# Taking GpSimd's low parts and state sums of the second mixer over to VectorE

## The chip, the cores and the metric

The kernel runs on one core of one Trainium2 chip. The metric is the device time of one execution in microseconds (us), and the time before is the median of three runs. The engines are TensorE (PE in the rows, PEld for its weight loads), VectorE (DVE), ScalarE (ACT), GpSimd (POOL) and SyncE (SP), which issues nearly all transfers here. Each engine takes its instructions in program order; engines wait for one another through semaphores.

## The reference, cut to what matters

The reference is an encoder trunk of two layers over 512 positions of width 1024, in float32. Layer 0 has a mixer of windowed attention and gated linear attention; layer 1 has the second mixer, which is the place of this change. Both are followed by cross-attention into 256 memory tokens and a gated feed-forward block.

```python
def mixer_cd(hn, w_in, w_out, ...):                     # the second mixer
    u_c, h_d = split_sizes(hn @ w_in, (C_WIDTH, 2 * D_WIDTH))
    y_f = s5_scan(u, ...)                                # a linear recurrence, forward
    y_b = flip(s5_scan(flip(u), ...))                    # and backward
    y = y_f + y_b + d_skip * u_c
    z = gelu(y)
    o_c = z * sigmoid(z @ w_glu + b_glu)
    o_d = conformer_conv(h_d, conv_w, ...)               # 31 taps, layer norm, silu
    return concatenate([o_c, o_d]) @ w_out
```

What is computed stays the same under the change: `a - b` and `a + b` of the same tiles are done on another engine.

## The kernel before, in words

**Weights in two parts.** Every large product is done with operands that are split into a high and a low part. `wload` (line 194) takes a raw block of 128x1024 weights (`wr`, fetched by line 147 through SP, 3 buffers), rounds it on ScalarE to the high part `wh` (line 201), and subtracts that from the raw block on VectorE, or on the engine that it is given, to get the low part `wl` (line 202). `mm3` then issues three matmuls for each 128x128 block: line 206 (high weights, high input), line 207 (high weights, low input) and line 208 (low weights, high input). So the first two can start once `wh` is there, and the third waits for `wl`. (Where the weights are the moving operand, as in the memory's value projection, line 207 is the one that reads `wl`.) `wh` and `wl` have two buffers each, and a raw block is free for the next transfer when both parts have been made.

**The second mixer.** `mixer_cd` runs a table of small steps, `CD`, in the order written there; `pinned` keeps the first TensorE and SP instruction of each step in that order. On VectorE and ScalarE the order comes from a list scheduler that estimates durations, so it can move rows there when an instruction changes its engine. The steps that matter here:

- `u`, `v`, `g` and `k`: products with the weights of the input projection (`half0` and `half1`) and with the memory's key and value weights (`vstep`, `kstep`). Each takes one block of weights through `wload`. The numbers in `LPOOL` name the blocks whose low part GpSimd makes.
- `c`, `C`, `s`, `x`: the linear recurrence of one group, forward (d = 0) and backward (d = 1). `c_` multiplies the input with the table on TensorE, copies it out on ScalarE, swaps its halves with two transfers, rotates it (lines 1380 to 1382), scans it (lines 1384 and 1386) and rotates it back (lines 1387 and 1388). `s_` has SP swap the halves of the result with four transfers (lines 1394 and 1395), and SP takes them in order with all other transfers: what stands behind them, the next weights among it, is issued only when line 1388 of both directions has ended. `x_` (line 1402) adds the two halves to the state `xp`; the numbers in `XPOOL` name the sums that GpSimd makes.
- `q`: taps of the convolution on VectorE (line 1463), 60 in all, which nothing on TensorE waits for soon.
- `V` and `G`: the gate and value of the convolution (lines 1440, 1445 and 1447), whose result TensorE transposes in `A` (line 1336).
- `N`: the layer norm of the convolution. VectorE adds up squares (line 1520), TensorE sums them over partitions (line 1522), ScalarE and VectorE make the factor from it (lines 244 to 247), VectorE applies it (line 1576), and the result, split into `cm` and `cst` tiles, is the second half of the input of the output projection.

The functions that take the two tables, and what calls them:

Of the kernel before, what the change touches and what calls it, by code (L numbers as in the profile page):

```python
# [75 lines left out]
S5_EVERY = 3  # L76
RAW = ((1, 3), (1, 5))
NPRE = 2
LPOOL, XPOOL = (5, 6, 7, 15, 18, 19, 20, 22, 24, 26), (1, 2, 6)
WAHEAD = 2  # L80
NQ = 2
CD = """
# [1651 lines left out]
```

## Time and profile before

| | |
|---|---|
| median of 3 runs | 1613.68 us (1609.65 to 1622.86) |
| the profiled execution | 1613.46 us, its span 1611.7 us |
| mean granted TensorE clock | 0.984 |
| busy, share of the span | PE 97%, PEld 81%, DVE 67%, ACT 44%, POOL 22% |
| the second mixer | about 861 us to 1100 us of the span |

The span runs from the first to the last instruction; 1.8 us of the execution's time lie outside it. All positions below are microseconds from the start of the span. A row of the timeline gives the start, the duration, the engine, the line, the operation, the output and its inputs, and, in square brackets, how long the engine sat idle before it and for whom.

### The profile page before, as it was taken

What the parts mean: (1) busy time and instruction counts of PE and PEld (TensorE: products, weight loads), DVE (VectorE), ACT (ScalarE), POOL (GpSimd) and SP (SyncE); (2) the same over time, 40 slices, a digit from 0 to 9 for tenths busy, and PEclk for the clock granted to TensorE, in tenths of its full rate; (3) what the DMA queues carried; (4) which work ended last, traced back from release to release, by engine and by line L of the source; (5) the groups of instructions that cost most, each with busy time, mean ns of one, the idle gap of its engine ahead of it and who ended that gap; (6) DMA issues with size and microseconds to landing.
All of it is one profiled execution on the core that took longest, in us unless ns stands there. A gap on an engine that the chain in (4) does not pass through costs nothing. (4 is left out here: it accounts for less than half of the span.)

```text
span 1611.7 us, 20961 instructions
## 1 busy us (share of the span) xinstructions
PE 1562.1 (97%) x8036; PEld 1307.9 (81%) x8036; DVE 1077.3 (67%) x1479; ACT 708.3 (44%) x1089; POOL 358.7 (22%) x367
## 2 busy tenths in 40 slices
PE   8999999999999999999999988989999999999997
PEld 6787889888888787777788877978888888888887
DVE  7576766466568789579746997375745766636644
ACT  5464755354444443234336342374534444414423
POOL 8411000000059853553510111110000101100101
PEclk9999999999999999999999998999999999999998
DMA  5322333231223335435454685452302322232331
GB/s 178 109 72 86 118 105 118 66 121 63 66 80 100 111 111 152 144 116 164 126 166 172 218 276 172 150 177 91 106 27 79 105 97 100 92 105 92 89 109 64
DMA packets 76117, 189.11 MB, mean 117 GB/s; under 512 B 8368, under 2 KB 27440, under 8 KB 76016
## 3 DMA queue, kind: packets, MB, share of 16 engines
q1 hardware_dynamic: 75376, 186.58, 36.1%
q8 instruction: 63, 1.03, 0.3%
q0 software_dynamic: 320, 1.05, 0.2%
q14 instruction: 38, 0.31, 0.1%
q10 hardware_dynamic: 320, 0.13, 0.0%
HBM read 162.43 MB, written 19.01 MB: 113 GB/s over the span
## 5 line engine op out<-in xcount | busy, mean ns | idle before, releaser
L201 ACT ACTIVATE wh<-wr 128x1024 fp32r<-128x1024 f32 (+1 forms) x229 | 239.2, 1045 | 430.3 <-PE mm L207 324.2
L208 PE MATMUL mm<-hg,wl 128*128 128x512 f32 x1000 | 394.9, 395 | 12.3 <-DVE wl L202 10.9
L206 PE MATMUL mm<-hg,wh 128*128 128x512 f32 x1000 | 399.2, 399 | 4.6 <-ACT wh L201 4.6
L207 PE MATMUL mm<-hg,wh 128*128 128x512 f32 x1000 | 393.6, 394 | 0.0
L202 DVE TENSOR_TENSOR wl<-wr,wh 128x1024 fp32r<-128x1024 f32 (+1 forms) x219 | 285.7, 1305 | 73.7 <-ACT wh L201 71.6
L208 PEld LDWEIGHTS mm<-hg,wl 128*128 128x128 f32 x1000 | 190.3, 190 | 56.6 <-DVE wl L202 13.7
L206 PEld LDWEIGHTS mm<-hg,wh 128*128 128x128 f32 x1000 | 190.7, 191 | 46.5 <-ACT wh L201 5.0
L207 PEld LDWEIGHTS mm<-hg,wh 128*128 128x128 f32 x1000 | 190.4, 190 | 40.4 <-issue 1.4
L208 PE MATMUL mm<-g,wl 128*128 128x512 f32 x324 | 126.7, 391 | 3.2 <-DVE wl L202 3.1
L206 PE MATMUL mm<-g,wh 128*128 128x512 f32 x324 | 126.9, 392 | 0.0
L207 PE MATMUL mm<-g,wh 128*128 128x512 f32 x324 | 126.2, 389 | 0.0
L976 POOL TENSOR_TENSOR t<-t,t 128x512 f32<-128x512 f32 x22 | 28.9, 1315 | 427.6 <-ACT t L182 427.6
L968 DVE TENSOR_TENSOR u<-mm,R 128x512 f32<-128x512 f32 x88 | 60.3, 688 | 73.8 <-PE mm L208 73.6
L970 ACT ACTIVATE t<-u,vt 128x512 f32<-128x512 f32 x88 | 70.8, 807 | 42.9 <-DVE u L968 42.6
L986 DVE TENSOR_TENSOR h<-mm,h 128x512 f32<-128x512 f32 x40 | 27.6, 691 | 87.7 <-PE mm L208 87.7
L971 DVE SCALAR_TENSOR_TENSOR t<-u,vt,t 128x511 f32<-128x511 f32 x88 | 77.8, 885 | 7.9 <-ACT t L970 7.9
L972 DVE SCALAR_TENSOR_TENSOR t<-u,vt,t 128x511 f32<-128x511 f32 x88 | 76.8, 872 | 4.0 <-DMA dct<-tr 1.4
L208 PEld LDWEIGHTS mm<-g,wl 128*128 128x128 f32 x324 | 60.8, 188 | 16.8 <-DVE wl L202 4.0
L182 ACT ACTIVATE t<-t 128x512 f32<-128x512 f32 x44 | 27.8, 632 | 102.3 <-DVE t L972 102.2
L207 PEld LDWEIGHTS mm<-g,wh 128*128 128x128 f32 x324 | 60.8, 188 | 12.5
L206 PEld LDWEIGHTS mm<-g,wh 128*128 128x128 f32 x324 | 60.9, 188 | 12.4
L202 POOL TENSOR_TENSOR wl<-wr,wh 128x1024 fp32r<-128x1024 f32 x10 | 25.3, 2531 | 148.4 <-ACT wh L201 148.4
(522 smaller groups left out, 3020.2 us busy)
## 6 DMA issues: line engine op xcount, KB each, us to landing
wr<-in_w_up SPq DMA_DIRECT2D x88, 512.0 KB
wr<-in_w_dn SPq DMA_DIRECT2D x32, 448.0 KB
wr<-in_w_ab SPq DMA_DIRECT2D x16, 512.0 KB
wr<-in_w_xv SPq DMA_DIRECT2D x16, 512.0 KB
wr<-in_w_xk SPq DMA_DIRECT2D x16, 512.0 KB
wr<-in_w_xq SPq DMA_DIRECT2D x16, 512.0 KB
wr<-in_w_xo SPq DMA_DIRECT2D x16, 512.0 KB
wr<-in_w_dn SPq DMA_DIRECT2D x16, 512.0 KB
```

The costliest lines, as they stand in the source:

```text
L182: tabbed(A.activation(dst, src, fn, **kw))
L201: A.activation(H[:, :n], raw[:, :n], AF.Copy)
L202: (eng or V).tensor_tensor(L[:, :n], raw[:, :n], H[:, :n].bitcast(F32), ALU.subtract)
L206: PE.matmul(ps, lH, rH, start=start, stop=False)
L207: PE.matmul(ps, lH, rL, start=False, stop=False)
L208: PE.matmul(ps, lL, rH, start=False, stop=stop)
L968: V.tensor_tensor(u, ps, R, ALU.mult)
L970: A.activation(t, u, AF.Identity, scale=vc(f"cw{l}", 44 + i), bias=vc(f"cb{l}", i))
L971: V.scalar_tensor_tensor(t[:, 1:], u[:, :S - 1], vc(f"cw{l}", i), t[:, 1:], op0=ALU.mult, op1=ALU.add)
L972: V.scalar_tensor_tensor(t[:, :S - 1], u[:, 1:], vc(f"cw{l}", 88 + i), t[:, :S - 1], op0=ALU.mult, op1=ALU.add)
L976: (V if l == 0 else G).tensor_tensor(res[1], res[1], res[0], ALU.mult)
L986: V.tensor_tensor(h[c], ps, h[c], ALU.add)
```

## The change

Two tables of numbers become empty:

```diff
@@ -76,7 +76,7 @@
 RAW = ((1, 3), (1, 5))
 NPRE = 2
-LPOOL, XPOOL = (5, 6, 7, 15, 18, 19, 20, 22, 24, 26), (1, 2, 6)
+LPOOL, XPOOL = (), ()
 WAHEAD = 2
 NQ = 2
```

With them, ten low parts of weights (line 202, 128x1024) and three sums of scanned states (line 1402, 128x512) go from GpSimd to VectorE. GpSimd keeps its few memsets (lines 1273 to 1278) in this mixer. SP's 460 rows stay as they are. TensorE and ScalarE have the same rows as before, with some of them in another order, and VectorE has 13 rows more. Three places follow.

VectorE in the scan of the third group: `T_1276` and `T_1280` are its two directions, `dv_7578` is the convolution's sum over taps, and `wl_7908` is a low part of the input projection's weights.

```order
 L1382 TENSOR_TENSOR T_1276_7726<-T_1276_7726,T1s_7727 128x512
 L1327 TENSOR_TENSOR uT_7802<-mm_7777,R_7356 128x512
+L202 TENSOR_TENSOR wl_7908<-wr_7771,wh_7907 128x1024
+L1463 SCALAR_TENSOR_TENSOR dv_7578<-dv_7424,vt,dv_7578 128x506
 L1382 TENSOR_TENSOR T_1280_7749<-T_1280_7749,T1s_7750 128x512
+L1384 SCALAR_TENSOR_TENSOR T1s_7727<-rt_7714,T_1276_7726 128x512
 L1463 SCALAR_TENSOR_TENSOR dv_7578<-dv_7424,vt,dv_7578 128x507
-L1384 SCALAR_TENSOR_TENSOR T1s_7727<-rt_7714,T_1276_7726 128x512
```

The low part now stands between the two directions' sums, and the rows of the scan are behind it. Two of the three state sums (`xp_7309` and `xp_7308`) come into VectorE's rows near here in the same way, one ahead of this piece and one behind it.

TensorE at the sum over partitions of the layer norm, line 1522 (`sc_8853`), among the key products of the memory (`mm_8989`, `mm_9022`). Before:

```order
L206 MATMUL mm_8989<-mg_7487,wh_8985 128x256
L207 MATMUL mm_8989<-mg_7487,wh_8985 128x256
L1522 MATMUL sc_8853<-T_1459_8838,ones 128x512
L206 MATMUL mm_9022<-mg_7487,wh_9018 128x256
L207 MATMUL mm_9022<-mg_7487,wh_9018 128x256
L208 MATMUL mm_8989<-mg_7487,wl_8986 128x256
```

Now:

```order
L207 MATMUL mm_8989<-mg_7765,wh_8985 128x256
L208 MATMUL mm_8989<-mg_7765,wl_8986 128x256
L1522 MATMUL sc_8853<-T_1459_8838,ones 128x512
L206 MATMUL mm_9022<-mg_7487,wh_9018 128x256
L207 MATMUL mm_9022<-mg_7487,wh_9018 128x256
L208 MATMUL mm_9022<-mg_7487,wl_9019 128x256
```

The sum over partitions now comes behind the whole product `mm_8989`, 22 matmuls later.

VectorE behind it, where the layer norm's factor is made and applied; `wl_9128` and `wl_9147` are low parts of the output projection's first two blocks:

```order
 L245 SCALAR_TENSOR_TENSOR T1s_9199<-sc_8853,T1s_9199 128x512
 L246 TENSOR_SCALAR T1s_9199<-T1s_9199 128x512
+L202 TENSOR_TENSOR wl_9128<-wr_9125,wh_9127 128x1024
 L247 TENSOR_TENSOR dg_9197<-T_1523_9198,T1s_9199 128x512
+L851 TENSOR_TENSOR kraw_9077<-mm_9083,Rm_8117 128x256
+L202 TENSOR_TENSOR wl_9147<-wr_9144,wh_9146 128x1024
 L1576 TENSOR_TENSOR dv_7578<-dv_7578,dg_9197 128x512
 L1576 TENSOR_TENSOR dv_7841<-dv_7841,dg_9197 128x512
```

Both low parts now stand ahead of the four products of line 1576; before, they came behind them.

## Rows read from the trace of the kernel before

**Rows 1.** The page, part 1: busy us (share of the span) and instructions.

```profile
PE 1562.1 (97%) x8036; PEld 1307.9 (81%) x8036; DVE 1077.3 (67%) x1479; ACT 708.3 (44%) x1089; POOL 358.7 (22%) x367
```

**Rows 2.** Windows of the mixer: length, busy by engine, granted clock, DMA.

```profile
950.00:970.00 20.00, 13.84 (x70) 9.98 (x69) 19.96 (x30) 9.51 (x17) 4.89 (x2) 0.93 0.89 324
970.00:990.00 20.00, 20.00 (x138) 18.14 (x139) 9.60 (x13) 4.49 (x6) 0.00 (x0) 0.90 0.21 52
990.00:1010.00 20.00, 16.62 (x88) 13.16 (x87) 19.96 (x25) 6.67 (x10) 4.28 (x2) 0.91 0.66 234
...
1080.00:1100.00 20.00, 20.00 (x82) 16.32 (x82) 10.26 (x13) 9.74 (x13) 0.00 (x0) 0.92 0.48 175
sum 260.00, PE 244.01 PEld 206.60 DVE 187.81 ACT 118.48 POOL 30.21; mean PE 16.27 PEld 13.77 DVE 12.52 ACT 7.90 POOL 2.01
```

**Rows 3.** Waits of TensorE from 860 to 1080: total us, times, longest.

```profile
PE mm L206 <- ACT wh L201: 3.5, 1, 3.5
PE mm L208 <- POOL wl L202: 3.3, 2, 1.8
PE tp L1336 <- DVE dv L1447: 2.8, 1, 2.8
PE mm L208 <- DVE wl L202: 1.8, 1, 1.8
PE sc L1522 <- DVE T L1520: 1.7, 1, 1.7
```

**Rows 4.** Lines 202 and 1402 in the mixer: ns minimum/median/maximum.

```profile
L202 DVE TENSOR_TENSOR wl<-wr,wh x18: 1203/1219/1590, 871.1 to 1071.5; 128x1024 fp32r<-128x1024 f32 x18
...
L202 POOL TENSOR_TENSOR wl<-wr,wh x10: 2353/2399/3380, 879.7 to 1068.1; 128x1024 fp32r<-128x1024 f32 x10
...
L1402 DVE TENSOR_TENSOR xp<-T,X2s x5: 672/677/1769, 903.5 to 1006.7; 128x512 f32<-128x512 f32 x5
```

**Rows 5.** Timeline of GpSimd, three of its 13 operations.

```profile
903.47 1.28 POOL L1402 TENSOR_TENSOR xp<-T,X2s 128x512 f32<-128x512 f32 x1 [21.31 <-DMA X2s<-T1s]
913.82 3.38 POOL L202 TENSOR_TENSOR wl<-wr,wh 128x1024 fp32r<-128x1024 f32 x1 [9.08 <-ACT wh L201]
...
1000.25 2.62 POOL L202 TENSOR_TENSOR wl<-wr,wh 128x1024 fp32r<-128x1024 f32 x1 [30.48 <-ACT wh L201]
```

**Rows 6.** Timeline of VectorE at the same moments and between them.

```profile
903.52 1.77 DVE L1402 TENSOR_TENSOR xp<-T,X2s 128x512 f32<-128x512 f32 x1
...
915.51 2.24 DVE L1382 TENSOR_TENSOR T<-T,T1s 128x512 f32<-128x512 f32 x1
...
927.23 1.78 DVE L1463 SCALAR_TENSOR_TENSOR dv<-dv,vt,dv 128x511 f32<-128x511 f32 x1
...
935.96 0.73 DVE L1463 SCALAR_TENSOR_TENSOR dv<-dv,vt,dv 128x501 f32<-128x501 f32 x1
...
1000.54 2.86 DVE L1463 SCALAR_TENSOR_TENSOR dv<-dv,vt,dv 128x504 f32<-128x504 f32 x1
1003.33 1.74 DVE L1447 SCALAR_TENSOR_TENSOR dv<-dg,dv 128x512 f32<-128x512 f32 x1
...
1059.06 2.62 DVE L1520 TENSOR_TENSOR T<-T,X2s 128x512 f32<-128x512 f32 x1 [0.17 <-ACT X2s L1519]
```

**Rows 7.** Timeline at the late block of weights: SP, ScalarE, TensorE.

```profile
958.23 0.46 SPq L1394 DMA_DIRECT2D X2s<-T1s  x1
...
966.08 1.06 ACT L201 ACTIVATE wh<-wr 128x1024 fp32r<-128x1024 f32 x1 [3.32 <-DMA wr<-in_w_cd]
...
969.83 0.80 PE L208 MATMUL mm<-hg,wl 128*128 128x512 f32 x1 [1.42 <-POOL wl L202]
```

**Rows 8.** The chain of waits, in order of time: start, us, what.

```profile
1070.89 0.12 PE mm L206
...
1079.49 0.23 PE mm L208
...
1081.23 0.43 PE mm L207
```

## The prediction, put on record before the result was known

> **What bounds the kernel now.** The page's first part says that TensorE is busy for 97% of the span and VectorE for 67% [rows 1], so the kernel as a whole is TensorE's, and an engine that is freed or loaded elsewhere counts only where TensorE stands still. I therefore read the windows of the second mixer next. From 860 to 1100 us there are 260.00 us less 244.01 busy, 16 us, in which TensorE does nothing, and in the windows that hold most of them VectorE is the full engine: 19.96 of 20 us from 950 to 970, and again from 990 to 1010 [rows 2]. This is the stage to look at, not VectorE's 67%. The waits of TensorE name what it stood still for: a high part of weights (3.5 us), low parts from GpSimd (3.3), the gated value of the convolution from line 1447 (2.8), a low part from VectorE (1.8), the last sum of squares (1.7) [rows 3]. That makes 13.1 of the 16 us.
>
> Last I laid the timelines of GpSimd and VectorE side by side, because the change turns on them. GpSimd needs 2.40 us for a low part where VectorE needs 1.22 [rows 4]. While GpSimd runs, the VectorE row that falls into it grows: the state sum at 903.52 takes 1.77 us where its median is 0.68; a sum of the same size at 915.51 takes 2.24 and ends when GpSimd's row of 913.82 is over; a tap at 1000.54 takes 2.86 where one takes 0.73 [rows 4 to 6]. So GpSimd's work here is not beside VectorE's but in it. It works the other way as well: GpSimd's low part at 913.82, among VectorE's rows, takes 3.38 us [rows 5].
>
> **The change, part by part.** Ten low parts at 1.22 and three sums at 0.68 are 14.2 us more rows on VectorE [rows 4], against the time by which rows no longer grow. What matters is the sum on the three paths that end in a wait of TensorE.
>
> Place 1, from 900 to 970. TensorE waits for a high part that ScalarE makes at 966.08, and ScalarE had waited 3.32 us for the block of weights [rows 7]. That block is late because SP issues it behind the swaps of the scanned states; the last two were issued from 958.23 on [rows 7], once line 1388 had ended, and VectorE had then been full since 900. On VectorE up to there, the change takes away the growth of three rows: 1.77 − 0.68 = 1.09, 2.24 − 0.68 = 1.56 and 1.78 − 0.73 = 1.05, together 3.70 us [rows 4, 6]. It puts in one low part and two sums, 1.22 + 2 × 0.68 = 2.58 [rows 4]. So the swaps, the block of weights and the high part come 1.1 us earlier: 966.08 becomes 965.0. The high part is there 1.06 later, at 966.0, and VectorE makes the low part in 1.22, at 967.3, where TensorE's first matmul with it started at 969.83 [rows 7]. The gain is **2.6 us**. It holds the 1.4 us wait for GpSimd's low part. Bounds: 1.1 if VectorE is not free when the high part is there, 3.5 + 1.4 = 4.9 if both waits vanish.
>
> A rule bears on this. The Trainium skill, "SBUF — State Buffer", section "Who interferes with whom", says that a VectorE instruction with two SBUF inputs and a GpSimd instruction that reads SBUF exclude each other for the whole instruction, and that whichever starts first holds the other up. By it the sum of 915.51 is held until GpSimd's end at 913.82 + 3.38 = 917.20, so for 1.69 us where the rows give 1.56 [rows 5, 6]; the one at 903.52 for 1.23 where they give 1.09. Put on three rows, the rule would make place 1 some 0.4 us better. The same rule speaks against the change where VectorE starts first: there GpSimd pays and VectorE loses nothing, as GpSimd's 3.38 us in part show. The sum here goes by the rows.
>
> Place 2, from 990 to 1010. TensorE waits 2.8 us for line 1447 [rows 3]. That row takes 1.74 instead of 0.68, and the tap in front of it 2.86 instead of 0.73 [rows 4, 6]: 1.06 + 2.13 = 3.2 us of growth right ahead of the wait, while the low part and the state sum that take GpSimd's place stand behind line 1447 in VectorE's new order. The gain is the whole wait, **2.8 us**. Bounds: 0 if a transfer ahead of the scan sets the time, 2.8.
>
> Place 3, from 1058 to 1080. Three waits lie here: 1.7 for line 1520, 1.8 for GpSimd's second low part, 1.8 for VectorE's low part behind the products of line 1576 [rows 3], 5.3 in all. The first goes, as line 1520 took 2.62 us [rows 6] and TensorE now has 22 matmuls ahead of line 1522. The second goes, as the low part is made in half the time. The third goes, as the low part now stands ahead of line 1576. Something is late in their place: line 1522 comes 22 matmuls of 0.12 us [rows 8] later, 2.6, less the 1.7 that it no longer waits, so 1.0 us later, and the layer norm behind it with the `cm` tiles that the output projection needs. The low part ahead of line 1576 adds up to 1.2 to that [rows 4], but TensorE gets ten matmuls of the second block to do first, 10 × 0.23 = 2.3 us [rows 8], so I count the 1.0 alone: **4.3 us**. Bounds: 5.3, and 0 if the `cm` tiles come no earlier than before and TensorE, ahead by 5.3, waits for them.
>
> The other moves cost nothing: from 1010 to 1050 TensorE has no wait in the list of [rows 3] and VectorE stands idle, so two low parts more fit in; the memsets of GpSimd stay. SP's queue is in the same order, and its weight transfers that waited for GpSimd to release a raw block can only be earlier.
>
> The granted clock is the other half. The windows at 0.93, 0.90, 0.91 and 0.92 [rows 2] are stretches at 1.2 GHz within 2.4 GHz: twice the missing share of 20 us, so 2.8 + 4.0 + 3.6 + 3.2 = 13.6 us, in which matmuls step 0.43 instead of 0.23 us [rows 8]. Half of it, 6.8 us, is work lost. Each of these stretches follows one of the waits above. Whether shorter waits spare TensorE the fall I can't read from a row: 0 to 6.8, and I take 0, since some wait stays at place 1.
>
> Sum: 2.6 + 2.8 + 4.3 = 9.7 us off the profiled execution's 1613.46 gives 1603.8, so **1604 us**. That execution stands 0.2 us below the median, so no correction is needed between them.
>
> **The rivals.** *The clock comes back too.* If all waits end short enough, the 6.8 us are gained as well: 1613.5 − 9.7 − 6.8 = 1597.0. For it: waits of 1.7 and 1.8 us at 1060 and 1070 left no stretch at 1.2 GHz before 1080. Against: place 1 keeps most of its 3.5 us wait for weights.
>
> *The gain is given back.* Place 1 hangs on a transfer, and place 3 on a layer norm that starts later; if the block of weights lands at the old time and the `cm` tiles come no earlier, place 2 alone counts: 1613.5 − 2.8 = 1610.7. For it: DMA engines are 89% busy from 950 to 970 [rows 2]. Against: ScalarE's 3.32 us wait came right behind a late issue.
>
> *VectorE becomes the bound, and the kernel slower.* If rows grow for a reason that stays (VectorE's own inputs, not GpSimd), the change only adds work to a full engine: 2.58 us ahead of the swaps at place 1, and 1.22 ahead of line 1520, so 1613.5 + 3.8 = 1617. It decides if fewer than 2.58 of the 3.70 us of growth vanish. Against it: every long row named above lies within a row of GpSimd.
>
> That the change doesn't do what it says is excluded by the new order, with 13 rows more on VectorE.
>
> **How the numbers follow.** Forecast 0.52, the clock too 0.18, given back 0.24, slower 0.06. The forecast's own range runs from 1600, with half of the clock's 6.8, to 1608, where one of the places gives nothing. The range from **1597 to 1611** reaches to the two neighbours' times; it leaves out the slower case and those halves of the neighbours' cases that lie beyond their times, somewhat less than 0.06 + 0.09 + 0.12, so about 2 in 10. About 1% is what a measurement of this kernel can tell from no change, here below 1597.5 or above 1629.8. Faster by over 1%: 0.12, two thirds of the clock's case. Within 1%: 0.86. Slower by over 1%: 0.02, since the slower case ends at 1617.
>
> **What would show it.** In the changed profile no row of lines 1463, 1382, 1402, 1447 and 1520 in this mixer lasts over 1.5 us, and all 28 low parts there are VectorE's at 1.2 us. TensorE's waits for GpSimd and for line 1447 are gone, those for a high part are below 3.5 us, and its idle time from 860 to 1100 falls from 16 us to some 6. The forecast is wrong if long VectorE rows stay without GpSimd beside them, or if new waits of TensorE for `cm` tiles or for transfers stand where the old ones were.

## The result, and the profile after

| | before | after |
|---|---|---|
| median of 12 runs each, same chip | 1617.35 us (1609.37 to 1623.37) | 1605.11 us (1598.00 to 1615.55) |
| after to before, 95% interval | | 0.9939 (0.9919 to 0.9958) |
| the profiled execution, its span | 1613.46, 1611.7 us | 1605.85, 1604.1 us |
| mean granted clock | 0.984 | 0.988 |

The kernel is faster by 0.61%, which is 9.8 us. The interval runs from 0.42% to 0.81%, 7 to 13 us, and the two medians of the table lie 12.2 us apart, so the time by itself says little about single places. The page's first part, after, answers to [rows 1]:

```profile
PE 1558.4 (97%) x8036; PEld 1303.9 (81%) x8036; DVE 1072.0 (67%) x1492; ACT 707.6 (44%) x1089; POOL 327.3 (20%) x354
```

VectorE has 13 rows more and is busy for 5.3 us less. Lines 202, 1402 and 1463 of VectorE in the mixer after (ns minimum/median/maximum), beside [rows 4], show why: no row is long any more, where before one sum took 1.77 us and one tap 2.86 [rows 6]. The longest row of lines 1382, 1447 and 1520 there takes 0.71 us.

```profile
L202 DVE TENSOR_TENSOR wl<-wr,wh x36: 1201/1224/1239, 864.0 to 1111.2; 128x1024 fp32r<-128x1024 f32 x36
...
L1402 DVE TENSOR_TENSOR xp<-T,X2s x8: 684/692/707, 906.6 to 1007.7; 128x512 f32<-128x512 f32 x8
...
L1463 DVE SCALAR_TENSOR_TENSOR dv<-dv,vt,dv x60: 721/742/769, 902.1 to 1012.6; 128x497 f32<-128x497 f32 x4, 128x498 f32<-128x498 f32 x4, 128x499 f32<-128x499 f32 x4, 128x500 f32<-128x500 f32 x4
```

TensorE's waits after, from 860 to 1100 us, to be read against [rows 3] (before, nothing stood between 1080 and 1100):

```profile
PE mm L207 <- DVE wl L202: 4.7, 3, 2.5
PE mm L206 <- ACT wh L201: 2.3, 2, 1.2
PE tp L1336 <- DVE uT L1327: 1.0, 1, 1.0
PE mm L208 <- DVE wl L202: 0.5, 1, 0.5
```

The waits for GpSimd, for line 1447 and for line 1520 are gone, the longest wait for a high part fell from 3.5 to 1.2, and 5.2 us for low parts from VectorE stand where before there were 2.4, the 1.8 of [rows 3] and 0.6 at place 2.

Windows of a fixed place don't compare, since the mixer starts at another time in each execution. I cut it at events: from VectorE's last row of line 986 ahead of it, to ScalarE's first row of line 1491 (place 1 lies in this window), to the next one (place 2), to the fourth, and to the eighth row of line 279, which adds up the output projection (place 3). Columns: length, busy time (x count) of PE, PEld, DVE, ACT and POOL, granted clock, DMA share, GB/s. Before:

```profile
860.74:981.58 120.84, 113.53 (x649) 93.70 (x647) 104.50 (x149) 53.93 (x84) 13.93 (x12) 0.97 0.63 218
981.58:1012.15 30.57, 27.19 (x180) 23.49 (x181) 24.48 (x31) 9.05 (x15) 4.28 (x2) 0.94 0.59 192
1012.15:1041.35 29.20, 29.20 (x230) 26.69 (x230) 8.04 (x8) 10.71 (x14) 7.10 (x3) 1.00 0.50 171
1041.35:1123.55 82.20, 76.90 (x397) 65.06 (x398) 52.31 (x67) 45.20 (x60) 4.90 (x2) 0.98 0.39 134
sum 262.81, PE 246.82 PEld 208.94 DVE 189.32 ACT 118.89 POOL 30.21; mean PE 61.71 PEld 52.23 DVE 47.33 ACT 29.72 POOL 7.55
```

After:

```profile
863.10:982.77 119.67, 112.75 (x649) 93.23 (x647) 101.55 (x155) 53.81 (x84) 0.32 (x6) 0.99 0.65 220
982.77:1011.78 29.01, 27.18 (x180) 23.63 (x180) 21.75 (x31) 9.09 (x14) 0.00 (x0) 0.94 0.62 202
1011.78:1042.18 30.40, 30.40 (x240) 27.91 (x241) 10.36 (x13) 11.66 (x16) 0.00 (x0) 1.00 0.49 180
1042.18:1115.75 73.57, 73.57 (x389) 62.46 (x388) 50.65 (x69) 43.71 (x60) 0.00 (x0) 1.00 0.42 143
sum 252.65, PE 243.90 PEld 207.24 DVE 184.31 ACT 118.28 POOL 0.32; mean PE 60.98 PEld 51.81 DVE 46.08 ACT 29.57 POOL 0.08
```

The mixer takes 252.65 us instead of 262.81: 10.2 us, about as much as was timed for the whole kernel. Two columns tell how: length less PE is TensorE's idle time, and the share that the clock lacks, times the length, is what the stretches at 1.2 GHz within 2.4 GHz cost. Idle time goes from 7.3, 3.4, 0 and 5.3 to 6.9, 1.8, 0 and 0, so by 7.2 us. The clock's cost goes from 3.6 + 1.8 + 1.6 = 7.0 to 1.2 + 1.7 = 2.9, so by 4.1; with the clock rounded to 0.01 this is good to about 1 us. Idle and busy time add up to the length, and TensorE's busy time fell by 2.9 us (246.82 to 243.90) for the same work, so 2.9 is the other measure of the clock's part. The 1.2 us that the third window grows are ten more matmuls of the memory's key products (230 and 240 in all), which moved into it out of the fourth.

### The profile page after: what moved, and what is told of

It is laid out like the page before. It is cut to its first block, busy times and chain, and to the rows that moved or that the text cites. A ratio compares the mean times of both kernels' runs of the same rounds, so it can differ in the third digit from the quotient of the medians.

```text
span 1604.1 us, 20956 instructions
## 1 busy us (share of the span) xinstructions
PE 1558.4 (97%) x8036; PEld 1303.9 (81%) x8036; DVE 1072.0 (67%) x1492; ACT 707.6 (44%) x1089; POOL 327.3 (20%) x354
## 4 chain that ended last, share of the span: by engine, by line
PE 70%; DVE 13%; POOL 6%; DMA 4%; ACT 3%; issue 3%; SPq 1%; ACTq 0%; DVEq 0%; POOLq 0%
PE mm L206 20%; PE mm L208 20%; PE mm L207 20%; DVE wl L202 2%; PE mm L737 2%; PE sc L1489 1%; DVE t L972 1%; DMA T1s<-T 1%; DVE t L971 1%; PE tp L724 1%; DVE t L976 1%; POOL t L1139 1%; PE sc L208 1%; PE sc L206 1%; PE sc L207 1%
## 5 line engine op out<-in xcount | busy, mean ns | idle before, releaser
L202 DVE TENSOR_TENSOR wl<-wr,wh 128x1024 fp32r<-128x1024 f32 (+1 forms) x229 | 296.2, 1294 | 76.4 <-ACT wh L201 74.4
L986 DVE TENSOR_TENSOR h<-mm,h 128x512 f32<-128x512 f32 x40 | 27.6, 691 | 87.8 <-PE mm L208 87.7
L206 PEld LDWEIGHTS mm<-g,wh 128*128 128x128 f32 x324 | 60.9, 188 | 12.2
L279 DVE TENSOR_TENSOR h<-mm,h 128x512 f32<-128x512 f32 x32 | 21.7, 688 | 46.2 <-PE mm L208 46.2
```

The costliest lines, as they stand in the source:

```text
L202: (eng or V).tensor_tensor(L[:, :n], raw[:, :n], H[:, :n].bitcast(F32), ALU.subtract)
L206: PE.matmul(ps, lH, rH, start=start, stop=False)
```

## The experiments

**How steady these numbers are: e10 and e8.** Each kernel was run again, without an edit, for a second profile.

> The kernel before once more, for a second profile of it. If the stage accounting is right, the idle time of TensorE comes out as in the first profile within 1.5 us for each place: some 7 in the first (to the first line 1491), 3.4 in the second (to the next line 1491), 5.3 in the last (from the fourth line 1491), however the mixer's start is shifted.

> The changed kernel once more, beside the others and with a second profile. The first gave 10.2 us less in the mixer from its entrance to the last sum of its output projection, 1.3 at place 1, 1.6 at place 2 and 7.4 at place 3, where I had 2.6, 2.8 and 4.3. If that split belongs to the kernel, it shows again to within 0.5 us; if it is the luck of one execution (the granted clock falls in steps), it moves by 1 us or more while the sum stays near 10. Ratio 0.994.

The kernel before, again, in the same windows:

```profile
871.43:992.50 121.07, 113.61 (x649) 93.63 (x647) 104.57 (x149) 53.92 (x84) 14.21 (x12) 0.97 0.62 218
992.50:1024.97 32.47, 28.77 (x180) 25.05 (x180) 25.41 (x32) 8.99 (x14) 4.33 (x2) 0.89 0.54 181
...
1054.17:1134.35 80.18, 76.80 (x397) 65.44 (x398) 52.42 (x67) 45.29 (x60) 4.92 (x2) 0.98 0.40 135
sum 262.92, PE 248.39 PEld 210.84 DVE 189.16 ACT 118.90 POOL 30.56; mean PE 62.10 PEld 52.71 DVE 47.29 ACT 29.73 POOL 7.64
```

The kernel after, again:

```profile
871.29:992.87 121.58, 114.14 (x649) 94.12 (x648) 101.47 (x155) 53.84 (x85) 0.32 (x6) 0.97 0.63 217
992.87:1019.39 26.52, 25.60 (x180) 22.61 (x180) 20.25 (x29) 8.99 (x14) 0.00 (x0) 1.00 0.66 220
...
sum 252.38, PE 243.97 PEld 207.16 DVE 184.20 ACT 118.20 POOL 0.32; mean PE 60.99 PEld 51.79 DVE 46.05 ACT 29.55 POOL 0.08
```

The mixer's length repeats within 0.3 us: 262.8 and 262.9 against 252.7 and 252.4. Its parts move by up to 2.5 us (place 2 of the kernel after: 29.01 and 26.52), so the first profile's split between the places was not the kernel's own. Place 3 idles 3.4 us in the second profile of before where it idled 5.3, a little outside the 1.5 that I had allowed. By the two profiles of each kernel, the change takes 0.2 us of idle time at place 1 (7.4 to 7.2), 2.2 at place 2 (3.5 to 1.4) and 4.3 at place 3 (4.3 to 0), together 6.7, and of the clock's cost 7.9 − 3.25 = 4.7, where TensorE's busy time shrinks by 3.7. Timed, e8 was at 0.9961 (0.9938 to 0.9984) of before, 1607.34 us.

**Which half of the change: e2 and e3.** e2 moves only the last two low parts (place 3), e3 everything but these.

```diff
-LPOOL, XPOOL = (), ()
+LPOOL, XPOOL = (5, 6, 7, 15, 18, 19, 20, 22), (1, 2, 6)    # e2
+LPOOL, XPOOL = (24, 26), ()                                # e3
```

> Only the low parts of the key blocks 24 and 26 go to VectorE, the two of place 3; the other eight and the three sums of states stay on GpSimd. The trace of the changed kernel, which gains 7.4 of its 10.2 us behind 1050 us, says 1613.5 - 7.4, ratio 0.9954. The prediction's own terms give place 3 4.3 us, ratio 0.9973. If the places hang together, so that place 3 gains only when the mixer before it is faster, 1.000.

> The complement: eight low parts and the three sums go to VectorE, and the blocks 24 and 26 stay on GpSimd. By the trace of the changed kernel 2.8 us are gained ahead of place 3, ratio 0.9983; by the prediction's terms 2.6 + 2.8 = 5.4 us, ratio 0.9967. With TensorE waiting for GpSimd's low part and line 1520 at place 3 as before.

e2: 0.9975 (0.9957 to 0.9992), 1610.33 us. e3: 0.9971 (0.9954 to 0.9987), 1610.88 us. The fourth window of e2:

```profile
1041.33:1116.05 74.72, 74.72 (x397) 63.81 (x398) 50.53 (x70) 44.79 (x60) 0.00 (x0) 1.00 0.43 145
```

In e3 it idles for 3.1 us, and two of the waits of before are there: 2.0 us for line 1520 and 0.4 for GpSimd's low part.

By time, then, two of the ten low parts make up nearly half of the gain, the whole of place 3, with its clock; the other eight with the three sums make up the rest. The two gains, 0.25% and 0.29%, add to 0.54%, where the whole change was timed at 0.61% and 0.39%; each is good to 0.17%. Both came out nearer to the forecast's own terms (0.9973 and 0.9967) than to the split of the first profile after (0.9954 and 0.9983), though e3's interval holds both.

By the length of the mixer the halves don't add: e2's takes 255.2 us and e3's 253.6, so 7.7 and 9.3 less than before, more together than the whole change's 10.3. The first windows, of e3 and of e6 (which comes below, and has after's rows with idle writes on GpSimd), show where this comes from:

```profile
871.25:988.90 117.65, 113.40 (x649) 93.85 (x647) 101.35 (x155) 54.04 (x84) 0.32 (x6) 0.97 0.64 224
858.25:977.08 118.83, 114.04 (x649) 94.28 (x648) 101.43 (x155) 54.04 (x85) 32.36 (x66) 0.97 0.63 222
```

TensorE idles for 4.3 and 4.8 us in them, where it idles for 6.9 and 7.4 in the two profiles of the kernel after, though VectorE has the same rows in the same order in all four up to the last swaps. What differs is told with place 1 below.

**Is it GpSimd's reading that holds VectorE up? e1, e5, e9 and e6.** In these, VectorE does all the work in the order of after, and GpSimd, in the ten places where it made low parts, works for nothing. e1 and e5 read the high part (two and six subtractions of 128x512), e9 does six on a tile of its own, e6 only writes (14 memsets of 128x512). All of them begin when the high part is there.

```diff
@@ wload
             (eng or V).tensor_tensor(L[:, :n], raw[:, :n], H[:, :n].bitcast(F32), ALU.subtract)
+            if ghost:                                            # e1; e5: 3 * (0, 512)
+                for o in (0, 512):
+                    G.tensor_tensor(gscr[0], H[:, o:o + 512].bitcast(F32), H[:, o:o + 512].bitcast(F32), ALU.subtract)
+            if ghost:                                            # e9
+                G.tensor_copy(gscr[0][:, :1], H[:, :1].bitcast(F32))
+                for _ in range(6):
+                    G.tensor_tensor(gscr[0], gscr[0], gscr[0], ALU.subtract)
+            if ghost:                                            # e6
+                G.tensor_copy(gscr[0][:, :1], H[:, :1].bitcast(F32))
+                for _ in range(14):
+                    G.memset(gscr[0], 0.0)
```

> The changed kernel with GpSimd given useless work again: for each of the ten blocks of weights that it used to split, it subtracts the high part from itself in two halves of 128x512 into a scratch tile that nothing reads. Every other row stands in the same order as in the changed kernel. Theory (GpSimd's reads of on-chip memory stretch VectorE's rows, and that is what the change took away): VectorE's rows of two on-chip inputs grow again by 1 to 2.5 us beside each half, and line 1388 at place 1, line 1447 at place 2 and line 1520 at place 3 come about 2 us later each, so 6 us or more of the 10 us come back: ratio to before 0.998, between 0.995 and 1.002. Rival (the gain is that low parts are made in 1.2 instead of 2.4 us, and the new order): nothing that anybody waits for has changed, ratio 0.994 as the changed kernel.

> The ghosts of the first experiment three times over: six useless subtractions of 128x512 on GpSimd for each of the ten blocks, about 78 us of it, all other rows in the changed kernel's order. The single dose gave 0.9959 with an interval from 0.9937 to 0.9981, which does not settle how much of the gain it takes back. Theory (reads by GpSimd stretch VectorE's rows, and VectorE's lateness is what TensorE waits for): VectorE loses some 4 to 6 us by each block, most of it from 900 to 1010 on the way to TensorE's waits, and the kernel becomes slower than before: ratio 1.003 or more. Rival (VectorE's stretched rows are hidden, and the gain came from low parts made faster and from the new order): 0.994 to 0.997.

> The kernel after the change, with GpSimd kept as busy as in e5_ghosts_x3 (six useless subtractions of 128x512 for each of the ten blocks), but on a scratch tile of its own, so that no high part of a weight is held by them. Theory (GpSimd instructions that read SBUF stretch VectorE's rows with two inputs): the same slowness as e5_ghosts_x3, 1.010 to 1.020 of before, with VectorE's subtractions of 128x1024 and taps stretched beside a GpSimd row. Rival (e5_ghosts_x3 was slow because its ghosts held the buffers of the high parts, and ScalarE's rounding stood behind them): about as after, 0.993 to 0.997, with no TensorE wait for a high part over what after has.

> A control: GpSimd is kept busy at the same moments and for as long or longer, but writes only: for each of the ten blocks it copies one column of the high part and then clears the scratch tile 14 times. All other rows in the changed kernel's order. Theory (it is GpSimd's reading that holds up VectorE's rows of two on-chip inputs): no row of VectorE grows over 1.3 us, ratio 0.994 as the changed kernel. Rival (any activity of GpSimd does, writes too): as the ghosts three times over, above 1.000.

e1: 0.9959 (0.9937 to 0.9981), 1609.30 us. e5: 1.0174 (1.0150 to 1.0197), 1641.63 us. e9: 1.0091 (1.0064 to 1.0117), 1631.13 us. e6: 0.9937 (0.9914 to 0.9960), 1602.71 us. The sums over the mixer's windows, e6:

```profile
sum 251.88, PE 245.39 PEld 208.30 DVE 184.28 ACT 118.42 POOL 80.09; mean PE 61.35 PEld 52.08 DVE 46.07 ACT 29.60 POOL 20.02
```

e1:

```profile
sum 253.12, PE 242.96 PEld 206.27 DVE 196.78 ACT 118.20 POOL 31.48; mean PE 60.74 PEld 51.57 DVE 49.20 ACT 29.55 POOL 7.87
```

e9:

```profile
sum 275.88, PE 251.70 PEld 211.55 DVE 219.12 ACT 118.52 POOL 93.59; mean PE 62.93 PEld 52.89 DVE 54.78 ACT 29.63 POOL 23.40
```

VectorE's rows are the same in the three and in after, and their busy time shows the hold-up by itself: 184.3 us in after and beside 80 us of GpSimd that mostly write, 196.8 beside 31 us that read, 219.1 beside 94 us of which 87 read. The timelines show it row by row. e9, VectorE and GpSimd (lines 204, 208 and 1471 are lines 202, the ghosts and 1463 in the numbering of after):

```profile
973.44 2.06 DVE L204 TENSOR_TENSOR wl<-wr,wh 128x1024 fp32r<-128x1024 f32 x1
974.50 7.66 POOL L208 TENSOR_TENSOR gscr<-gscr 128x512 bf16<-128x512 bf16 x5
...
976.87 7.92 DVE L1471 SCALAR_TENSOR_TENSOR dv<-dv,vt,dv 128x508 f32<-128x508 f32 x6
```

e6, the same rows of VectorE in GpSimd's memsets (line 1470 is line 1463):

```profile
956.85 7.52 POOL L208 MEMSET gscr<- 128x512 bf16 x13
957.32 1.21 DVE L204 TENSOR_TENSOR wl<-wr,wh 128x1024 fp32r<-128x1024 f32 x1
...
959.05 4.00 DVE L1470 SCALAR_TENSOR_TENSOR dv<-dv,vt,dv 128x508 f32<-128x508 f32 x6
```

The low part takes 2.06 and 1.21 us, the sum between 1.52 and 0.67, the six taps 7.92 and 4.00. The Trainium skill, "SBUF — State Buffer", section "Who interferes with whom", says that a VectorE instruction with two SBUF inputs contends with a GpSimd instruction that reads SBUF and not with one that only writes it; the 34.8 us of e9 and the 0.0 of e6 agree.

e9 lies just below the 1.010 to 1.020 that the theory gave and far from the rival's 0.997 at most: reading a tile that nobody waits for is enough to cost 23 us of mixer. The other part of e5's slowness fits its ghosts' hold on the buffers of the high parts (TensorE waits 11.6 us for high parts in e5 and 1.6 in e9, at the same busy time of VectorE), so e5 alone would have shown too much. e1 came between its two expectations, and it is the one that bounds the theory: 31.5 us of reading, as much as GpSimd was busy before (30.2), bring back 12.5 us of stretch, where before had 189.3 + 14.2 (ten low parts at 1.22, three sums at 0.68) − 184.3 = 19.2. Yet the mixer grows by only 0.6 us, and idle time is 10.2 us against 8.8 and 8.4. So in this profile two thirds of the stretch alone cost almost nothing, within the 2 us by which a place moves. That GpSimd's reading holds VectorE up is shown; that this hold-up is what the change won back is not. What e1 leaves over is the stretch at the wrong rows, low parts that took GpSimd 2.4 to 3.4 us, and the order of before, since e1 keeps the order of after. I did not separate these three further.

**What place 1 waits for: e4, e11, e7 and e12.** e4 issues the four swaps of line 1394 and 1395 from GpSimd. e11 has that and puts the step that loads the rotation tables (`L3`) behind the next block of weights. e7 leaves SP alone and puts eight of the steps of two taps behind the scans of the last group. e12 is e11 and e7 together. Moving the swaps also changes what the list scheduler makes of VectorE and ScalarE: in e4 and e11 the second row of line 1388 stands ahead of lines 1327 and 1431, as it did before the change, so the queue is not all that differs from after. The cuts from `CD` leave out what stays.

```diff
-                nc.sync.dma_start(xs[0:64], t1s[64:128])
-                nc.sync.dma_start(xs[64:128], t1s[0:64])
+                nc.gpsimd.dma_start(xs[0:64], t1s[64:128])       # e4, e11, e12
+                nc.gpsimd.dma_start(xs[64:128], t1s[0:64])
@@ CD, e11 and e12
-... q1 u3 s2 L3 q0 q1 f1 k1 l3 a3 ...
+... q1 u3 s2 q0 q1 f1 k1 l3 L3 a3 ...
@@ CD, e7 and e12
-... s2 L3 q0 q1 f1 k1 l3 a3 q0 q1 x2 k1 b3 q1 v3 q0 V3 Z2 c3 C3 q1 y2 q1 g3 w2 q1 G3 k1 m3 q1 f2 A3 s3 q1 Z2 k1 w3 x3 F2 q1 B3
-k1 k1 y3 Z3 w3 k1 f3 k1 Z3 k1 F3 N0
+... s2 L3 q0 f1 k1 l3 a3 q0 x2 k1 b3 v3 q0 V3 Z2 c3 C3 y2 g3 w2 G3 k1 m3 f2 A3 s3 Z2 k1 w3 x3 F2 B3 q1 k1 q1 k1 q1 y3 q1 Z3 q1 w3 q1 k1
+q1 f3 q1 k1 Z3 k1 F3 N0
```

> The changed kernel with the swaps of the scanned states (lines 1394 and 1395) issued by GpSimd, which is idle there, instead of SP. Theory (at place 1 the block of weights is late because SP issues it behind the swaps that wait for line 1388): the weights come 2 us or more earlier there, TensorE's waits for high and low parts from 960 to 975 fall from 5.3 us to under 2.5, and with some of the clock the ratio to before is 0.991. Rival (the transfers themselves are what is late, since the 16 engines are full there): the waits stay, ratio 0.994; and if GpSimd's issuing of transfers delays the swaps or stretches VectorE's rows, above 0.995.

> The kernel after the change, with the four swaps of scanned states on GpSimd's queue, and the last load of the rotation tables behind the next block of weights in the program's order, so that nothing which waits for line 1388 stands ahead of that block on SP's queue. Theory (place 1 still idles since SP's queue holds the weights back behind line 1388): TensorE's waits for a high part and a low part near 970 go, and the idle time of the first place falls from some 7 us to below 3.5; the time to 0.990 to 0.993 of before. Rival (the weights aren't what place 1 stands on: VectorE's own list is late there): idle of 5 us or more, 0.9935 to 0.996.

> The changed kernel with eight of the convolution's tap steps (16 taps of the second channel block, 10.5 us of VectorE) moved in the table of steps from 925 to 965 us to the stretch behind step F2, from 1012 us on, where VectorE is idle more than half of the time. Theory (what is left of TensorE's waits at places 1 and 2, 8.5 us in the changed kernel's trace, is VectorE's full stretch): these waits fall by 3 us or more and the ratio is 0.990 to 0.992. Rival (those waits hang on transfers, or the taps hold up VectorE's rows for TensorE behind 1012 instead): 0.994 to 0.996.

> e11_swaps_and_table with the eight tap steps of e7_taps_late also moved behind the scans. If both gains add: idle time of all places together below 3.5 us, 0.988 to 0.991 of before. If the taps' move already gave what the queue's move gives, as e7_taps_late: 0.992 to 0.993.

e4: 0.9937 (0.9915 to 0.9960), 1607.46 us, and its place 1 idles for 8.4 us, more than that of after. SP's queue in e4:

```profile
965.59 2.31 SPq L1363 DMA_DIRECT2D cst<-dct  x2
967.99 0.46 SPq L147 DMA_DIRECT2D wr<-in_w_cd  x1
```

The loads of the rotation tables stood behind the swaps, and their buffers are freed by line 1388, the very row that the swaps wait for. One wait had stood in front of another. The block of weights is issued 99.0 us after the mixer's start, 2.5 earlier than in after, but ScalarE starts its high part only at 107.6, as late as in after (107.5), since it is 8.6 us under way instead of 6.0; why it takes longer is not shown.

e11: 0.9915 (0.9886 to 0.9944), 1600.77 us. Its first window:

```profile
865.28:981.52 116.24, 111.07 (x649) 92.10 (x648) 98.71 (x152) 54.09 (x85) 6.67 (x18) 1.00 0.68 227
```

The block of weights is issued at 954.60, 89.3 us after the mixer's start, where after has it at 101.5 (964.60 − 863.10). All waits for a high part are gone in this profile, and the clock's cost with them. But 5.2 us stay idle, as the rival had it, for VectorE's own rows. TensorE's waits in this window:

```profile
PE tp L1336 <- DVE uT L1327: 2.4, 2, 1.9
PE mm L207 <- DVE wl L202: 2.4, 2, 1.7
```

So both were right in part: SP's queue held the high part back, and behind it VectorE's list is late.

e7: 0.9924 (0.9905 to 0.9943), 1602.08 us, mixer 247.5 us. Its place 2 has no idle time left, so what stayed there after the change hung on VectorE's taps. e12: 0.9908 (0.9882 to 0.9934), 1601.32 us; its mixer takes 245.5 us, of which TensorE is busy for 241.9, so its idle time is 3.6 us, at the edge of the 3.5 expected.

e7, e11 and e12 beat the kernel before. Their intervals overlap with those of the kernel after (0.9939 and 0.9961) and with one another's, so by time alone they can't be told from it or apart; their mixers are shorter than its 252.7 and 252.4 us, e12's most (245.5 against 247.5 and 247.2), in one profile of each.

## Why the prediction was right, and where it was not

The forecast was 1604 us, 9.7 us off; measured were 9.8, and 10.2 and 10.5 in the mixer. The sum was right; two of its terms were not, and they cancelled. (The 260.00 us of [rows 2] that it reads as 860 to 1100 run from 840; the first 20 of them hold no idle time, so its 16 us stand.)

- **Place 3, 4.3 us: right.** 4.3 by the two profiles of each (5.3 and 3.4 to 0), with no new wait: the layer norm that starts 22 matmuls later makes nobody wait. e2 gives it by itself.
- **Place 2, 2.8 us: right in kind, 2.2 measured.** The wait for line 1447 is gone, but a wait for a low part of VectorE, 0.6 and 0.9 us in the two profiles of before, is 1.8 and 0.9 in those of after; in e7, where taps moved away, it is gone.
- **Place 1, 2.6 us: the path failed; 0.2 measured in the two profiles of each kernel, though 2.6 to 3.1 in e3 and e6.** I had VectorE full up to line 1388, so that rows which stop growing bring the swaps, the weights and the high part 1.1 us earlier, and I costed only the low part behind the late block as VectorE's. Two rows of before, of VectorE and ScalarE:

```profile
957.52 0.68 DVE L1388 TENSOR_TENSOR T1s<-T1s,cst 128x512 f32<-128x512 f32 x1
...
956.89 1.06 ACT L201 ACTIVATE wh<-wr 128x1024 fp32r<-128x1024 f32 x1 [2.19 <-DMA wr<-in_w_xv]
```

VectorE's, ScalarE's, SP's and TensorE's timeline after, against these and [rows 6, 7]:

```profile
906.63 0.69 DVE L1402 TENSOR_TENSOR xp<-T,X2s 128x512 f32<-128x512 f32 x1 [0.52 <-DMA X2s<-T1s]
...
914.01 0.69 DVE L1380 TENSOR_TENSOR T<-T,cst 128x512 f32<-128x512 f32 x1 [1.85 <-DMA T1s<-T]
...
959.58 0.68 DVE L1327 TENSOR_TENSOR uT<-mm,R 128x512 f32<-128x512 f32 x1
...
960.25 1.21 DVE L1431 SCALAR_TENSOR_TENSOR uT<-uT,vt,sc 128x512 f32<-128x512 f32 x1
961.11 0.59 ACT L1337 ACTIVATE at<-tp 64x512 f32<-64x512 f32 x1 [5.00 <-PE tp L1336]
961.37 0.69 DVE L1388 TENSOR_TENSOR T1s<-T1s,cst 128x512 f32<-128x512 f32 x1
961.61 1.04 ACT L201 ACTIVATE wh<-wr 128x1024 fp32r<-128x1024 f32 x1
...
962.09 0.46 SPq L1394 DMA_DIRECT2D X2s<-T1s  x1
...
962.70 0.72 PE L206 MATMUL mm<-wh,mg 128*128 128x512 f32 x2 [1.19 <-ACT wh L201]
...
964.60 0.38 SPq L147 DMA_DIRECT2D wr<-in_w_cd  x1
964.61 1.22 DVE L202 TENSOR_TENSOR wl<-wr,wh 128x1024 fp32r<-128x1024 f32 x1
...
965.88 0.79 PE L207 MATMUL mm<-wl,mg 128*128 128x512 f32 x1 [2.45 <-DVE wl L202]
...
970.58 1.06 ACT L201 ACTIVATE wh<-wr 128x1024 fp32r<-128x1024 f32 x1 [6.93 <-DMA wr<-in_w_cd]
```

  Four things stood against it.
  1. VectorE, no longer held up, came early to rows whose transfers were not there: it waits 0.52, 1.85 and, once more at line 1380, 0.23 us. I had put these 2.6 us at nothing.
  2. In the new order lines 1327 and 1431, 0.68 + 1.21 us, stand ahead of the second row of line 1388; three taps, 3 × 0.73 us, went behind it in return (34 of them stand ahead of it where there were 37). With the forecast's own terms, −3.70 + 2.58 + 1.89 − 2.19 + 2.60, the row comes 1.2 us later. From the mixer's start, the swaps behind it are issued at 962.09 − 863.10 = 99.0 us, before at 958.23 − 860.74 = 97.5, so 1.5 us later instead of 1.1 earlier. The high part follows, at 107.5 instead of 105.3, as its block of weights is also 6.0 us under way where it was 5.4.
  3. ScalarE now makes the high part of the block ahead behind line 1337, 98.5 us after the mixer's start where it was 96.2, and TensorE waits 1.19 us for it.
  4. The low part of that block, which had been GpSimd's, now stands in VectorE's list: its high part is there at 961.61 + 1.04 = 962.65, but a sum and two taps go first, it starts at 964.61, and TensorE waits for it 2.45 us, where before that block brought no wait.

  In the first window, waits of 1.2 us for a high part and 1.4 for GpSimd went, and 3.3 for low parts of VectorE came. For this reason the idle time from 860 to 1100 fell to 8.7 us, not to the 6 that I had named.

  How much of this shows depends on the transfers. e3, the row of 914.01:

```profile
919.85 0.69 DVE L1380 TENSOR_TENSOR T<-T,cst 128x512 f32<-128x512 f32 x1 [0.28 <-DMA T1s<-T]
```

  The transfers that this row waits for are issued at 44.1 to 44.3 us after the mixer's start in after, e8, e3 and e6 alike, but the row starts at 50.9 and 50.7 in the first two and at 48.6 in e3 and e6. There VectorE waits for transfers for 0.5 and 0.3 us in all up to line 1388, and the swaps are issued at 96.6 and 96.5, 0.9 to 1.0 us ahead of before and close to the 1.1 of the forecast. The high part still comes at 105.4 and 105.0, hardly earlier than before, and what place 1 gains in them, 2.6 to 3.1 us against the 7.4 of before, is not won on the forecast's path. Why the same transfers land 2 us apart stays open.
- **The clock, 0 of 6.8 us: too low.** By the two profiles of each, its cost in the mixer is 7.9 before and 3.25 after, so 4.7 came back; by TensorE's busy time it was 3.7. Only at place 3 is it gone in both profiles after, as the rival had it for all places; place 1 costs 1.2 in one of them and 3.6 in the other, place 2 1.7 and 0. So shorter waits went with fewer stretches at 1.2 GHz, in e11 with none; I had put this at nothing.

What the forecast had too much at places 1 and 2 (2.4 and 0.6) was made up by what it left out for the clock (3.7 to 4.7); that the two were of nearly one size is luck. VectorE as the bound, and slower, did not come: without GpSimd beside them no VectorE row is long. The time's range held since its two ends were the neighbours' sums, the clock's among them.

## What to carry to other kernels

An engine's long rows beside another engine's rows cost time only where somebody waits for just those rows: e1 brought two thirds of the stretch back for 0.6 us of mixer, e9 nearly twice the stretch for 23. When rows are freed ahead of a wait, look in the new order at every row between them and the row that releases it, and at the transfers that the freed engine then comes to early. And when a transfer is late at the head of a queue, see what the one behind it waits for, before moving the first.

## What the runs showed of the hardware that was not expected

The two profiles of before differ by 10.8 us of span, yet their mixers by 0.1. The difference lies ahead of it, and most of it in one window. Before:

```profile
100.00:200.00 100.00, 97.61 (x588) 79.95 (x588) 71.14 (x123) 64.10 (x109) 10.55 (x7) 1.00 0.33 100
```

Before again:

```profile
100.00:200.00 100.00, 97.22 (x541) 80.38 (x540) 63.86 (x107) 56.02 (x93) 10.76 (x7) 0.91 0.29 90
```

TensorE is as busy, but at a granted clock of 0.91 instead of 1.00, 9 us of work. Of the 14 profiles of this study, seven have 0.91 in this window and seven 1.00, though all these kernels do the same work there, and the kernels before and after each have one of either kind. The timed runs of one kernel fall apart likewise: of e8's twelve, six have a mean granted clock of 0.980 to 0.983 and take 1608.0 to 1616.0 us, six have 0.987 to 0.990 and take 1599.8 to 1606.6. That is as large as the effect studied here, and the reason why the length of a stage between its own events told more than a span.
